# Moving the second layer's modulation out of the first layer's work queue, and dropping the zeroed accumulator banks of the scans

## The chip, the cores and the metric

One program runs on one core of one Trainium2 chip. The metric is device time in microseconds of a whole execution; lower is better. Below, PE is TensorE (matmuls), PEld its weight loads, DVE is VectorE, ACT is ScalarE, POOL is GpSimd, and SP is SyncE, whose queue issues almost all loads.

## The reference, cut to what matters

Two layers run over 256 context and 256 latent tokens of width 2048. Each layer modulates a normalised input, projects it, runs four token mixers (A and C are attention, B and D are bidirectional scans), merges them and projects back:

```
for l in range(2):
    shift, scale, gate = split(silu(c) @ w_mod[l] + b_mod[l], 3)     # the modulation; once more with c_ctx
    h = rms(x, norm_g[l]) * (1 + scale) + shift
    p = h @ w_in[l]
    y = [mixer_a(p), mixer_b(p), mixer_c(p), mixer_d(p)]             # B: RWKV scan, D: gated delta scan
    x = x + gate * (sum_i sigmoid(p_g @ g_up[l][i] + g_b[l][i]) * (y[i] @ w_br[l][i]) @ w_out[l])
return rms(x, final_g)
```

The modulation depends on c alone and not on x, so the second layer's may be computed at any time before it is used: shift and scale at the start of layer 1, gate at its end.

## The kernel before

Features lie on the 128 partitions in 16 tiles, the 512 tokens along the free axis. Products with big weights are done as three float32r matmuls of 128x128 by 512 columns: `weights` (L371) loads 256 KB into a "wr" buffer (5 of them) by SP, ScalarE casts it to "wh", VectorE takes the remainder "wl" (4 buffers each).

**Modulation.** `w_mod` of a layer is 12 chunks of 512 columns; chunks 0 to 3 give shift, 4 to 7 scale, 8 to 11 gate. `mod_unit` (L471) does one unit: four loads of 256 KB from `in_wmod`, and four float32 matmuls of 128x32 by 512 columns, each to another strip of 32 partitions of one bank. Sixteen units are a group of four chunks. With `acc` the group accumulates in one bank; without it each unit takes a new "big" bank and VectorE adds it to "ms". After the last unit four small matmuls and four additions put the result into `mod`.

**Order of the work.** Long products are generators in a queue. `small` (L259) is called for each matmul of the scans, adds its cost times `rho` to a debt, and pumps filler from the queue until the debt is paid. `rho` is from the table `RHO`, by layer and by stage (B or D). The filler of layer 0 is 45 projections (56, less the 11 that the first stage makes), then the merges of B, D, A and C, 16 output tiles each. `MODL` says which modulation units go along: for layer 0 the gate's 16 units of layer 0, and all 48 of layer 1. One unit is enqueued behind each projection (L437 to L441), the others run after every second tile of the merges (L1376). Both take "wr" buffers for their loads. The modulation for shift and scale of layer 0 runs in the first stage (`mods`, L1509), with 16 buffers "mr" of its own, between the first projections. Instructions stand on each engine's queue in an order fixed at build time, and each engine works its queue in that order. It isn't the order of the code throughout: work that is ready earlier can be put ahead.

**Output projection and boundary.** `out_proj` (L1381) splits the merged rows and then, for each of 16 tiles, loads x, runs 4 weight loads of 256 KB with 48 matmuls of 512 columns, adds the residual and (in layer 0) stores the latent half to `x1`. `rms_rows` (L514) then sums squares over the partitions and gives the row norms; `build_h` (L522) normalises and modulates the 16 tiles; three projections (Bw, Bk0, Bv0) start at once, a quarter of the 16 tiles at a time, in three banks.

**Scans.** Each of the 4 heads or head pairs of B and D accumulates its two directions in the one bank "acc". `zero_acc` (L326) opens that bank with a matmul of 512 columns by a tile of zeros, "zr", and all later matmuls add.

Of the kernel before, what the change touches and what calls it, by code (L numbers as in the profile page):

```python
# [9 lines left out]
F32 = mybir.dt.float32  # L10
F32R = mybir.dt.float32r
# [161 lines left out]
MXB = 3  # L173
NL2 = 3
MODS = (2, 3)
MODL = (((0, 8, 12), (1, 0, 12)), ())
NMAIN = 6
MORE = 5
STACK = (True, False)
PLAIN = ('', 'BA')  # L180
SIDE = (2.0, 1.8)
RHO = (((1.75,) * 4, (1.75,) * 4), ((1.8,) * 4, (1.4,) * 4))
QUANT = 2600.0
STEP = 1050.0
BG = (3, 3, 4, 10, 10)
# [2 lines left out]
class Kern:  # L188
# [134 lines left out]
    def tmp(s, n=512):  # L323
        return s.tl(s.rp, [128, T], "raw")[:, 0:n]

    def zero_acc(s):  # L326

        ps = s.psa.tile([128, 512], F32, tag="acc", name=s.nm("acc"))
        s.mm(ps, s.zr, s.zr[:, 0:1].to_broadcast([128, 512]), True, False)
        return ps  # L330

    def rsqrt(s, v, n):

# [97 lines left out]
    def enqueue_proj(s, names, mods=0):  # L431

        for name in names:
# [4 lines left out]
            for _ in range(mods):  # L438
                u = next(s.modq, None)
                if u is not None:  # L440
                    s.enqueue(u, s.mod_gen(u))  # L441

    def mod_gen(s, u):
        s.mod_unit(*u, [(s.wp, "wr")])
        return
        yield
# [21 lines left out]
        s.nc.vector.memset(s.s32, 0.0)  # L468
        s.ts(s.s32[:, :, 6:8], th, 0.5, None, ALU.mult)

    def mod_unit(s, l, chunks, u, pools, acc=False):  # L471


        nc = s.nc
        i, nch = u // 4, len(chunks)
        first, last = u == 0, u == 4 * nch - 1
        raws = []
        for g in range(4):
            pool, tag = pools[g % len(pools)]
            raw = s.tl(pool, [128, 512], tag)  # L480
            nc.sync.dma_start(raw, s.i["wmod"][l, chunks[i], u % 4 * 4 + g])
            raws.append(raw)
        if first or not acc:
            s.mps = s.big()
        ps = s.mps
        for g in range(4):
            s.mm(ps[32 * g:32 * g + 32, :], s.s32[:, u % 4 * 4 + g, 6 - 2 * i:38 - 2 * i], raws[g],
                 not acc or first, not acc or last)
        if last if acc else first:
            s.ms = s.tl(s.rp, [128, 512], "ms")  # L490
            nc.scalar.copy(s.ms, ps)
        elif not acc:
            s.tt(s.ms, s.ms, ps, ALU.add)
        if last:
            par, mod = s.lp[l]
            bo = _PO["bm"][0]
            w = 2 * nch
            p2 = s.big()
            for f in range(4):
                s.mm(p2[:, w * f:w * f + w], s.ms[:, f * 128:(f + 1) * 128], s.c("sel", 0, w))  # L500
            pv = p2[:, 0:4 * w].rearrange("p (f i c) -> p i f c", f=4, c=2)
            for i, n in enumerate(chunks):
                s.tt(mod[:, n * 4:n * 4 + 4, :], pv[:, i], wide(par[:, bo + n * 4:bo + n * 4 + 4], 2), ALU.add)
# [461 lines left out]
    def b_scan(s, J, d):  # L965
        nc = s.nc
        pool, t0 = s.bst["pool"], s.bst["t0"]
# [2 lines left out]
        vt = J["vt"]  # L970
        HS = (slice(0, 64), slice(64, 128))
        if d == 0:
            J["y"] = s.zero_acc()
        yps = J["y"]
        pc = None
        S = None
        for st in range(8):
# [28 lines left out]
            if c >= c0:  # L1006
                for R in HS:
                    o = yps[R, c * 64:c * 64 + 64]
                    s.mm(o, vt[R, c, :], AT[1][1][R, c, :], False, False)
                    if st > 0:  # L1010
                        s.mm(o, S[R, :], ar[R, c, 1, :], False, False)
                    s.mm(o, U[R, :], AT[0][1][R, c, :], False, d == 1 and st == 7)
# [231 lines left out]
    def d_scan(s, H):  # L1244
# [2 lines left out]
        k, kt, QD, sc, F = H  # L1247
        pool, t0 = s.dst["pool"], s.dst["t0"]
        m0 = t0 // 128
        ops_ = s.zero_acc()  # L1250
        S = [None, None]
        for st in range(4):
            ms = [s.ORDER2[d][st] for d in range(2)]
# [34 lines left out]
            for d, m in enumerate(ms):  # L1288
                if m >= m0:
                    o = ops_[:, tk[d]]  # L1290
                    if st > 0:
                        s.mm(o, S[d], sc[d][1][:, m * 128 - t0:m * 128 + 128 - t0], False, False)
                    s.mm(o, vn[d], QD[d][:, m - m0, :], False, d == 1 and st == 3)
            S = Sn
        return ops_

# [84 lines left out]
    def out_proj(s, xs_pool):  # L1381
# [10 lines left out]
            al.append(lo)  # L1392
        sqa = s.tl(xs_pool, [128, T], "sqa")[:, 0:n]
        xn = []
        for dt in range(KT):
            xo = s.tl(s.rp, [128, T], "po")[:, 0:n]
            nc.sync.dma_start(xo, s.i["xT"][dt] if l == 0 else s.x1[dt])
# [11 lines left out]
            s.sumsq(sqa, x, dt == 0)  # L1409
            if l == 0:  # L1410
                nc.sync.dma_start(s.x1[dt], x[:, CTX:])
            xn.append(x)
        return xn, sqa

# [7 lines left out]
    def open(s, ctx):  # L1422
# [9 lines left out]
        s.pss = ctx.enter_context(tc.tile_pool(name="pss", bufs=5 - MXB, space=MemoryType.PSUM))  # L1432
        s.psa = ctx.enter_context(tc.tile_pool(name="psa", bufs=1, space=MemoryType.PSUM))
        dr = ctx.enter_context(tc.tile_pool(name="dr", bufs=1, space=MemoryType.DRAM))
        s.zr = s.tl(s.cp, [128, 128], "zr0", F32R)
        z = s.tmp(128)
        s.nc.vector.memset(z, 0.0)
        s.nc.vector.tensor_copy(s.zr, z)
        s.cst = {}
        s.consts("cst", s.cp)  # L1440
        s.x1 = [dr.tile([128, CTX], F32, tag=f"x1_{k}", name=f"x1_{k}") for k in range(KT)]
# [43 lines left out]
    def run(s):  # L1485
        tc, nc = s.tc, s.nc
        with ExitStack() as ctx:
# [56 lines left out]
            for l in range(L):  # L1544
# [4 lines left out]
                with tc.tile_pool(name=f"xs{l}", bufs=1) as xp:  # L1549
                    xn, sqa = s.out_proj(xp)  # L1550
                    rsb = s.rms_rows(sqa, xp)
                    if l + 1 < L:
                        s.l = l + 1
                        s.par, s.mod = s.lp[l + 1]
                        s.build_h(xn, rsb)
                        names = ["Bw", "Bk0", "Bv0", "Br0", "Bk1"][:NL2]
                        banks = [s.bank() for _ in range(MXB)] + [s.scb((128, 512)) for _ in range(5 - MXB)]
                        s.filling = True
                        for g in range(4):
                            for ps, name in zip(banks, names):  # L1560
                                t0 = CTX if name[1] == "r" else 0
                                s.proj_part(ps[:, 0:T - t0], l + 1, name, t0, g)
                        for ps, name in zip(banks, names):
                            t0 = CTX if name[1] == "r" else 0
                            s.proj_park(ps[:, 0:T - t0], l + 1, name, t0)
                            s.done.add((l + 1, name))
# [22 lines left out]
```

## Time and profile before

| | us |
|---|---|
| median of 3 runs (2890.31 to 2902.11) | 2894.54 |
| the profiled execution | 2890.47 |
| its span | 2888.7 |
| PE busy, share of the span | 2740.9, 95% |
| DVE busy, share of the span | 1887.3, 65% |

The profiled execution is 1.8 us longer than its span, and 4.1 us under the median. In time order: the first stage to 174 us, layer 0's B scans to about 800, its D scans with both attentions to about 1395, the drain of merges to about 1541, the first output projection to 1735, the boundary to about 1790, then layer 1. Busy times are unions; two matmuls that overlap in the pipeline count once. A matmul's record is longer than the time it holds the engine, so costs are read from start to start.

### The profile page before, as it was taken

How to read it: one execution, taken by the hardware profiler on the slowest of the kernel's cores; microseconds unless marked ns; L12 is line 12 of the kernel's file. 1: busy time of each engine (PE TensorE's matmuls, PEld its weight loads, DVE VectorE, ACT ScalarE, POOL GpSimd, SP SyncE). 2: the span in 40 equal slices, each digit the busy share in tenths (PEclk: the TensorE clock that was granted, in tenths of full speed). 3: DMA queues.
4: the chain of work that ended last, by engine and by line, in shares of the span. 5: the costliest groups of instructions: out<-in, count | busy, mean ns of one | idle time of the engine just before them, and what ended most of it. 6: DMA issues, size and time to landing. Idle time of an engine off the chain costs nothing.

```text
span 2888.7 us, 52594 instructions
## 1 busy us (share of the span) xinstructions
PE 2740.9 (95%) x19454; PEld 2067.3 (72%) x19454; DVE 1887.3 (65%) x5302; ACT 1264.9 (44%) x2705; POOL 180.4 (6%) x436
## 2 busy tenths in 40 slices
PE   7998999999999999899999997999999999999897
PEld 3576566766667676666678886776777887877797
DVE  4337776656666767766555335777776677677775
ACT  3334333333244555555344225534433356455553
POOL 0000000000000101000000000001000001100000
PEclk9999999999999999999999998999999999899998
DMA  9753243433454434434634443323322453432465
GB/s 338 259 187 124 85 128 107 137 105 107 160 175 132 146 114 141 134 115 147 188 123 121 129 128 98 102 80 90 93 74 86 141 152 94 132 101 79 143 185 162
DMA packets 210049, 385.80 MB, mean 134 GB/s; under 512 B 24640, under 2 KB 37824, under 8 KB 209792
## 3 DMA queue, kind: packets, MB, share of 16 engines
q1 hardware_dynamic: 199872, 351.23, 39.6%
q0 software_dynamic: 9920, 31.20, 2.9%
q8 instruction: 153, 2.51, 0.4%
q14 instruction: 104, 0.85, 0.1%
HBM read 346.95 MB, written 35.39 MB: 132 GB/s over the span
## 4 chain that ended last, share of the span: by engine, by line
PE 71%; DVE 13%; ACT 5%; issue 5%; DMA 5%; POOL 0%; SPq 0%; DVEq 0%; ACTq 0%; POOLq 0%
PE big L283 47%; PE mx L283 12%; PE sc L283 6%; PE mx L305 3%; PE acc L283 3%; DVE wl L312 2%; DVE iX L312 1%; DMA wr<-in_win 1%; DVE it L312 1%; ACT raw L309 1%; ACT wh L376 1%; DVE raw L312 1%; DMA wr<-in_gup 1%; DMA wr<-in_wbr 1%; DMA po<-y 0%
## 5 line engine op out<-in xcount | busy, mean ns | idle before, releaser
L283 PE MATMUL big<-Rb,wh 128*128 128x512 f32 (+1 forms) x3280 | 1101.8, 365 | 14.7 <-ACT Rb L1317 5.5
L283 PE MATMUL big<-Ra,wh 128*128 128x512 f32 (+1 forms) x2128 | 780.5, 367 | 11.6 <-DVE po L315 7.7
L376 ACT CAST wh<-wr 128x512 fp32r<-128x512 f32 x712 | 438.4, 619 | 751.9 <-PE big L283 422.5
L283 PEld LDWEIGHTS big<-Rb,wh 128*128 128x128 f32 x3280 | 611.6, 192 | 119.3 <-ACT Rb L1317 9.9
L312 DVE TENSOR_TENSOR wl<-wr,wh 128x512 fp32r<-128x512 f32 x712 | 487.5, 688 | 286.9 <-ACT wh L376 276.5
L283 PE MATMUL big<-Ra,wl 128*128 128x512 f32 (+1 forms) x1616 | 595.2, 369 | 6.8 <-DVE wl L312 6.8
L283 PEld LDWEIGHTS big<-Ra,wh 128*128 128x128 f32 x2128 | 407.1, 191 | 106.7 <-issue 14.5
L283 PE MATMUL big<-Rb,wl 128*128 128x512 f32 (+1 forms) x1088 | 379.7, 349 | 0.9 <-DVE wl L312 0.9
L283 PEld LDWEIGHTS big<-Ra,wl 128*128 128x128 f32 x1616 | 309.5, 192 | 57.1 <-DVE wl L312 11.9
L283 PEld LDWEIGHTS big<-Rb,wl 128*128 128x128 f32 x1088 | 207.8, 191 | 26.6 <-DVE wl L312 1.8
L312 DVE TENSOR_TENSOR iX<-iX,it 128x60 f32<-128x60 f32 (+24 forms) x744 | 181.0, 243 | 15.5
L312 DVE TENSOR_TENSOR it<-iB,iX 128x60 f32<-128x60 f32 (+24 forms) x744 | 172.2, 231 | 15.3
L315 DVE SCALAR_TENSOR_TENSOR po<-po,big 128x512 f32<-128x512 f32 (+1 forms) x128 | 70.4, 550 | 81.3 <-PE big L283 72.9
L283 PE MATMUL big<-Rb,wr 128*128 128x256 f32 (+1 forms) x448 | 113.4, 423 | 5.0 <-DVE Ra L315 2.4
L309 ACT ACTIVATE po<-big,gb 128x512 f32<-128x512 f32 (+1 forms) x128 | 74.0, 578 | 93.8 <-PE big L283 79.9
L309 ACT ACTIVATE sw<-S,wc 128x64 f32<-128x64 f32 x96 | 33.4, 348 | 173.3 <-DVE S L315 149.7
L283 PE MATMUL big<-wr,s 128*32 128x512 f32 x512 | 97.4, 613 | 3.7 <-DVE ms L312 2.3
L283 PEld LDWEIGHTS big<-Rb,wr 128*128 128x128 f32 (+1 forms) x448 | 72.5, 182 | 25.9 <-issue 8.5
L283 PE MATMUL big<-mr,s 128*32 128x512 f32 x256 | 55.4, 638 | 17.8 <-DMA mr<-in_wmod 17.8
L283 PE MATMUL sc<-vt,AT 64*64 64x64 f32 x512 | 72.1, 238 | 0.0
L315 DVE SCALAR_TENSOR_TENSOR cz<-raw,par,cz 128x508 f32<-128x508 f32 (+3 forms) x96 | 67.1, 699 | 3.0 <-ACT cz L309 2.3
L626 DVE TENSOR_REDUCE mx<-mx 128x1 f32<-128x512 f32 (+1 forms) x96 | 57.1, 597 | 16.5 <-PE mx L283 15.2
(369 smaller groups left out, 4090.6 us busy)
## 6 DMA issues: line engine op xcount, KB each, us to landing
wr<-in_win SPq DMA_DIRECT2D x440, 256.0 KB, 2.7
wr<-in_wmod SPq DMA_DIRECT2D x256, 256.0 KB, 4.0
mr<-in_wmod SPq DMA_DIRECT2D x128, 256.0 KB, 5.2
wr<-in_wbr SPq DMA_DIRECT2D x128, 256.0 KB, 2.7
wr<-in_wout SPq DMA_DIRECT2D x128, 256.0 KB, 2.9
wr<-in_gup SPq DMA_DIRECT2D x64, 256.0 KB, 2.7
x<-in_xT SPq DMA_DIRECT2D x16, 256.0 KB, 5.4
po<-y SPq DMA_DIRECT2D x16, 256.0 KB, 3.3
```

Of the source, the lines that this page charges most:

```text
L283: s.nc.tensor.matmul(o, l, r, start=start, stop=stop)
L305: s.nc.tensor.transpose(o, i, s.c("id"))
L309: s.nc.scalar.activation(o, i, f, bias=bias, scale=scale, **k)
L312: s.nc.vector.tensor_tensor(o, a, b, op)
L315: s.nc.vector.scalar_tensor_tensor(o, a, sc, b, op0, op1)
L376: s.nc.scalar.copy(hi, raw)
L626: nc.vector.tensor_reduce(mx[:, hc], ps[:, 0:nk], AX.X, ALU.max)
```

## The change

- `MODL` keeps only the 16 units of layer 0's gate in the queue. The 48 units of layer 1 leave it.
- `next_mods` is a generator of these 48 units, in the order shift, scale, gate, all in the accumulating form, with "mr" buffers in the output projection's pool. Shift and scale take a bank of the "mx" pool, the gate one of the "big" pool.
- `out_proj` of layer 0 draws two units behind every tile, after the store of `x1`: 32 units, shift and scale.
- At the boundary eight units stand ahead of `build_h`, and two behind each of the four quarters of the first projections: 16 units, the gate.
- `zero_acc` becomes `acc_bank`: no matmul by zeros; the first matmul into the bank starts the accumulation. "zr" goes, with the instructions that make it.
- `RHO` for layer 0's D stage goes from 1.75 to 1.65.

```diff
--- before.py
+++ after.py
@@ -173,13 +173,13 @@
 MXB = 3
 NL2 = 3
 MODS = (2, 3)
-MODL = (((0, 8, 12), (1, 0, 12)), ())
+MODL = (((0, 8, 12),), ())
 NMAIN = 6
 MORE = 5
 STACK = (True, False)
 PLAIN = ('', 'BA')
 SIDE = (2.0, 1.8)
-RHO = (((1.75,) * 4, (1.75,) * 4), ((1.8,) * 4, (1.4,) * 4))
+RHO = (((1.75,) * 4, (1.65,) * 4), ((1.8,) * 4, (1.4,) * 4))
 QUANT = 2600.0
 STEP = 1050.0
 BG = (3, 3, 4, 10, 10)
@@ -323,11 +323,10 @@
     def tmp(s, n=512):
         return s.tl(s.rp, [128, T], "raw")[:, 0:n]
 
-    def zero_acc(s):
-
-        ps = s.psa.tile([128, 512], F32, tag="acc", name=s.nm("acc"))
-        s.mm(ps, s.zr, s.zr[:, 0:1].to_broadcast([128, 512]), True, False)
-        return ps
+    def acc_bank(s):
+
+
+        return s.psa.tile([128, 512], F32, tag="acc", name=s.nm("acc"))
 
     def rsqrt(s, v, n):
 
@@ -440,6 +439,13 @@
                 if u is not None:
                     s.enqueue(u, s.mod_gen(u))
 
+    def next_mods(s, pool):
+
+        for n in (0, 4, 8):
+            for u in range(16):
+                s.mod_unit(s.l + 1 if n < 8 else s.l, tuple(range(n, n + 4)), u, [(pool, "mr")], True, s.bank if n < 8 else None)
+                yield
+
     def mod_gen(s, u):
         s.mod_unit(*u, [(s.wp, "wr")])
         return
@@ -468,7 +474,7 @@
         s.nc.vector.memset(s.s32, 0.0)
         s.ts(s.s32[:, :, 6:8], th, 0.5, None, ALU.mult)
 
-    def mod_unit(s, l, chunks, u, pools, acc=False):
+    def mod_unit(s, l, chunks, u, pools, acc=False, bank=None):
 
 
         nc = s.nc
@@ -481,7 +487,7 @@
             nc.sync.dma_start(raw, s.i["wmod"][l, chunks[i], u % 4 * 4 + g])
             raws.append(raw)
         if first or not acc:
-            s.mps = s.big()
+            s.mps = (bank or s.big)()
         ps = s.mps
         for g in range(4):
             s.mm(ps[32 * g:32 * g + 32, :], s.s32[:, u % 4 * 4 + g, 6 - 2 * i:38 - 2 * i], raws[g],
@@ -495,7 +501,7 @@
             par, mod = s.lp[l]
             bo = _PO["bm"][0]
             w = 2 * nch
-            p2 = s.big()
+            p2 = (bank or s.big)()
             for f in range(4):
                 s.mm(p2[:, w * f:w * f + w], s.ms[:, f * 128:(f + 1) * 128], s.c("sel", 0, w))
             pv = p2[:, 0:4 * w].rearrange("p (f i c) -> p i f c", f=4, c=2)
@@ -970,7 +976,7 @@
         vt = J["vt"]
         HS = (slice(0, 64), slice(64, 128))
         if d == 0:
-            J["y"] = s.zero_acc()
+            J["y"] = s.acc_bank()
         yps = J["y"]
         pc = None
         S = None
@@ -1006,7 +1012,7 @@
             if c >= c0:
                 for R in HS:
                     o = yps[R, c * 64:c * 64 + 64]
-                    s.mm(o, vt[R, c, :], AT[1][1][R, c, :], False, False)
+                    s.mm(o, vt[R, c, :], AT[1][1][R, c, :], d == 0 and c == c0, False)
                     if st > 0:
                         s.mm(o, S[R, :], ar[R, c, 1, :], False, False)
                     s.mm(o, U[R, :], AT[0][1][R, c, :], False, d == 1 and st == 7)
@@ -1247,7 +1253,7 @@
         k, kt, QD, sc, F = H
         pool, t0 = s.dst["pool"], s.dst["t0"]
         m0 = t0 // 128
-        ops_ = s.zero_acc()
+        ops_, fresh = s.acc_bank(), True
         S = [None, None]
         for st in range(4):
             ms = [s.ORDER2[d][st] for d in range(2)]
@@ -1289,8 +1295,10 @@
                 if m >= m0:
                     o = ops_[:, tk[d]]
                     if st > 0:
-                        s.mm(o, S[d], sc[d][1][:, m * 128 - t0:m * 128 + 128 - t0], False, False)
-                    s.mm(o, vn[d], QD[d][:, m - m0, :], False, d == 1 and st == 3)
+                        s.mm(o, S[d], sc[d][1][:, m * 128 - t0:m * 128 + 128 - t0], fresh, False)
+                        fresh = False
+                    s.mm(o, vn[d], QD[d][:, m - m0, :], fresh, d == 1 and st == 3)
+                    fresh = False
             S = Sn
         return ops_
 
@@ -1392,6 +1400,8 @@
             al.append(lo)
         sqa = s.tl(xs_pool, [128, T], "sqa")[:, 0:n]
         xn = []
+        if l == 0:
+            s.modn = s.next_mods(xs_pool)
         for dt in range(KT):
             xo = s.tl(s.rp, [128, T], "po")[:, 0:n]
             nc.sync.dma_start(xo, s.i["xT"][dt] if l == 0 else s.x1[dt])
@@ -1409,6 +1419,8 @@
             s.sumsq(sqa, x, dt == 0)
             if l == 0:
                 nc.sync.dma_start(s.x1[dt], x[:, CTX:])
+                for _ in range(2):
+                    next(s.modn)
             xn.append(x)
         return xn, sqa
 
@@ -1432,10 +1444,6 @@
         s.pss = ctx.enter_context(tc.tile_pool(name="pss", bufs=5 - MXB, space=MemoryType.PSUM))
         s.psa = ctx.enter_context(tc.tile_pool(name="psa", bufs=1, space=MemoryType.PSUM))
         dr = ctx.enter_context(tc.tile_pool(name="dr", bufs=1, space=MemoryType.DRAM))
-        s.zr = s.tl(s.cp, [128, 128], "zr0", F32R)
-        z = s.tmp(128)
-        s.nc.vector.memset(z, 0.0)
-        s.nc.vector.tensor_copy(s.zr, z)
         s.cst = {}
         s.consts("cst", s.cp)
         s.x1 = [dr.tile([128, CTX], F32, tag=f"x1_{k}", name=f"x1_{k}") for k in range(KT)]
@@ -1552,6 +1560,8 @@
                     if l + 1 < L:
                         s.l = l + 1
                         s.par, s.mod = s.lp[l + 1]
+                        for _ in range(8):
+                            next(s.modn)
                         s.build_h(xn, rsb)
                         names = ["Bw", "Bk0", "Bv0", "Br0", "Bk1"][:NL2]
                         banks = [s.bank() for _ in range(MXB)] + [s.scb((128, 512)) for _ in range(5 - MXB)]
@@ -1560,6 +1570,8 @@
                             for ps, name in zip(banks, names):
                                 t0 = CTX if name[1] == "r" else 0
                                 s.proj_part(ps[:, 0:T - t0], l + 1, name, t0, g)
+                            for _ in range(2):
+                                next(s.modn)
                         for ps, name in zip(banks, names):
                             t0 = CTX if name[1] == "r" else 0
                             s.proj_park(ps[:, 0:T - t0], l + 1, name, t0)
```

## Rows read from the trace of the kernel before

**Rows 1.** The page: busy time by engine, and the last chain by engine.

```profile
PE 2740.9 (95%) x19454; PEld 2067.3 (72%) x19454; DVE 1887.3 (65%) x5302; ACT 1264.9 (44%) x2705; POOL 180.4 (6%) x436
...
PE 71%; DVE 13%; ACT 5%; issue 5%; DMA 5%; POOL 0%; SPq 0%; DVEq 0%; ACTq 0%; POOLq 0%
```

**Rows 2.** Busy in stretches: stretch, length, PE, PEld, DVE, ACT, POOL; clock, DMA share, GB/s.

```profile
800.00:1395.00 595.00, 562.10 (x3384) 408.69 (x3382) 420.17 (x1217) 306.67 (x706) 44.55 (x117) 0.98 0.44 138
1395.00:1541.00 146.00, 140.87 (x610) 106.45 (x611) 82.57 (x132) 57.28 (x92) 0.00 (x0) 0.99 0.47 146
1585.00:1735.00 150.00, 149.84 (x662) 123.73 (x660) 57.36 (x95) 42.85 (x69) 0.00 (x0) 1.00 0.43 130
1735.00:1768.00 33.00, 16.49 (x61) 13.08 (x61) 25.51 (x54) 25.84 (x52) 1.84 (x5) 0.69 0.10 31
```

**Rows 3.** Timeline, PE, layer boundary: start, length, engine, line, operation, [idle, releaser].

```profile
1745.79 0.80 PE L283 MATMUL mx<-Ra,wh 128*128 128x512 f32 x1 [3.53 <-ACT Ra L536]
...
1767.87 0.80 PE L283 MATMUL mx<-Ra,wh 128*128 128x512 f32 x1 [8.36 <-ACT wh L376]
...
1771.45 0.53 PE L283 MATMUL mx<-Ra,wl 128*128 128x512 f32 x1
```

**Rows 4.** Timeline, PE: units among scan matmuls and between projections.

```profile
570.27 1.06 PE L283 MATMUL big<-wr,s 128*32 128x512 f32 x8
571.27 0.33 PE L283 MATMUL sc<-vt,AT 64*64 64x64 f32 x2
...
764.63 1.07 PE L283 MATMUL big<-wr,s 128*32 128x512 f32 x8
...
777.20 1.06 PE L283 MATMUL big<-wr,s 128*32 128x512 f32 x8
```

**Rows 5.** Timeline, PE and DVE: merges with units (first two) and without.

```profile
1426.91 1.07 PE L283 MATMUL big<-wr,s 128*32 128x512 f32 x8
...
1436.95 1.06 PE L283 MATMUL big<-wr,s 128*32 128x512 f32 x8
...
1507.76 0.69 DVE L315 SCALAR_TENSOR_TENSOR po<-po,big 128x512 f32<-128x512 f32 x1 [0.73 <-PE big L283]
...
1511.84 0.69 DVE L315 SCALAR_TENSOR_TENSOR po<-po,big 128x512 f32<-128x512 f32 x1 [0.49 <-PE big L283]
```

**Rows 6.** Instructions on tile "ms": form, count, shortest, median, longest in ns.

```profile
L312 DVE TENSOR_TENSOR ms<-ms,big x60: 661/684/690, 251.3 to 1448.4; 128x512 f32<-128x512 f32 x60
```

**Rows 7.** Timeline, PE, first stage: units with buffers of their own.

```profile
110.06 1.06 PE L283 MATMUL big<-mr,s 128*32 128x512 f32 x8
...
114.00 1.07 PE L283 MATMUL big<-mr,s 128*32 128x512 f32 x8
```

**Rows 8.** Stretches, instructions on tile "s": PE, PEld, DVE; clock, DMA share, GB/s.

```profile
0.00:73.00 73.00, 28.26 (x104) 4.97 (x104) 0.75 (x2) 0.98 0.95 338
73.00:146.00 73.00, 19.68 (x104) 3.01 (x104) 0.00 (x0) 1.00 0.74 253
```

**Rows 9.** Timeline, SP's queue, first output projection.

```profile
1606.42 7.57 SPq L373 DMA_DIRECT2D wr<-in_wout  x4
1616.10 0.33 SPq L1411 DMA_DIRECT2D x<-x  x1
```

**Rows 10.** Timeline, PE: a bank of zeros and the matmul after it.

```profile
795.12 0.46 PE L283 MATMUL acc<-zr 128*128 128x512 f32 x1
795.41 0.39 PE L283 MATMUL big<-Ra,wh 128*128 128x512 f32 x1
```

**Rows 11.** Busy time of instructions on tile "big" in the D stage.

```profile
800.00:1395.00 595.00, 402.17 (x1622) 255.71 (x1620) 45.63 (x73) 30.97 (x48) 0.98 0.44 138
```

**Rows 12.** Loads of modulation weights: who waited for them; time to landing.

```profile
  PEld big L283: 11.3, 24
DMA to landing us min/median/max: 2.5/4.2/6.7
```

## Prediction

> **What bounds the kernel now.** I read the page first. TensorE (PE) is busy 95% of the span, and the chain that ended last lies on it for 71%; no other engine passes 72% [rows 1]. A share is a mean, so next came the busy time by stretch. In the first output projection PE is busy 149.84 of 150 us, 662 matmuls of 512 columns or 0.226 us each: that stretch is full. In the stretch with the D scans and both attentions PE is busy 562 of 595 us, in the drain of merges behind it 141 of 146 us. The layer boundary is the exception: 16.49 of 33 us, at a granted clock of 0.69 and a DMA share of 0.10 [rows 2]. PE's timeline shows why: after the last output tile PE waits for the row norms, does a burst of projections, then stands 8.36 us while ScalarE is still normalising the next tiles [rows 3]. What the change takes from the full stretches therefore comes back; what it puts into the output projection is paid; what it puts into the boundary may be free.
>
> **Units taken out of layer 0.** A modulation unit is 4 loads of 256 KB and 4 column-tiled matmuls, 8 records. 64 run in layer 0 from the queue: one behind each of 45 projections, 19 inside the merges. 48 of them (29 and 19) are the second layer's and leave.
> Price of one between projections: two units start 12.57 us apart with one projection of 48 matmuls between them [rows 4]. 48 x 0.2267 is 10.88, so the unit and what it upsets cost 1.69 us. It takes four of the five "wr" buffers, and the next weights come late. Where small scan matmuls stand on both sides, the unit costs only its own 1.00 us [rows 4]. Most lie between these, so I take 1.4: 29 x 1.4 = 40.6 us.
> Price of one in a merge: in the drain two units start 10.04 us apart, around two output tiles; without units one tile takes 4.08 us [rows 5]. So 10.04 - 8.16 = 1.88 us. Six of the 19 run in that drain (two stand in the rows): 11.3 us. The other 13 run beside scans and attention, where part of the upset meets other waits; I take 1.4, 18.2 us.
> Together 70 us back. Bounds: 48 x 1.00 = 48, and 29 x 1.69 + 19 x 1.88 = 84.7 us. VectorE also loses 45 of its 60 additions into "ms" at 0.684 us [rows 6], 31 us of an engine that isn't the bound; where PE waits for one, it is already in the 1.69 and 1.88, so nothing more is counted.
>
> **Units put into the output projection.** Two per output tile, 32 in all. They use 16 buffers of their own ("mr"), leave "wr" to the weights, and accumulate in one bank, so no addition follows each. The first stage has this form, one unit after every 12 or 24 matmuls: 3.94 us from unit to unit with 12 matmuls between [rows 7], so 3.94 - 2.72 = 1.22 us, with nothing upset behind it. In a pair the second saves the changes of tile form: 1.00 by [rows 4]. So 16 x 2.22 = 35.5 us. Bounds: 32 x 1.00 = 32, and 32 x 1.88 = 60 if they upset the weights as in the merges.
> The cover for their loads: each tile moves 1 MB of weights and 2 MB for units, some 0.4 MB of x besides. That is 3.5 MB in about 13.1 us, 267 GB/s. In the first stage the engines moved 253 GB/s at a share of 0.74, and 338 at most [rows 8]; I take the loads as hidden. Each load is also an issue on SP, which carries the weights and the store of x1. Over one tile SP issues four weight loads in 7.57 us and is then held for the next store [rows 9]; eight more issues of 0.33 us are 2.6 us of a period of 13. The end of each chunk group adds a copy, 8 small matmuls and 4 additions, as it did before in the queue: zero.
>
> **Units put into the boundary.** Eight ahead of the normalised tiles and eight between the projections. At 1.0 to 1.22 they are 16 to 19.5 us against 16.5 us of idle PE [rows 2]. Besides, the 8 intervals from 1767.87 to 1771.45 took 3.58 us, 0.45 each, which is the 1.2 GHz level, where 1.81 would do at 2.4 GHz [rows 3]; a PE with units in its gaps may skip this once or twice, 1.8 to 3.5 us back. Against it: only 4 units have buffers, so 12 or more of the 16 load after the last output tile, at 3.1 us each by 338 GB/s [rows 8], some 40 us beside the 55 us that the boundary lasts. New waits: a unit whose data is late holds every matmul behind it on PE, the norm statistics and projections among them; a load that waits for a buffer holds SP, and with it "win" weights and the first loads of layer 1. I take +4 us (a few units uncovered), bounds -3.5 (all covered, clock held) and +19.5 (none).
>
> **Bank of zeros.** Eight scans per layer open with one matmul of 512 columns; it holds PE 0.29 us from its start to the next and lasts 0.46 [rows 10]. 16 x 0.29 = 4.6 us back, bounds 3.6 (16 x 0.2267) and 7.4. The first real matmul now waits for the bank, later than the zeros did: zero.
>
> **Spacing 1.75 to 1.65 in the D stage.** 5.7% less filler per scan step. Work in "big" is 402 us there [rows 11], so up to 23 us of it moves into the drain. While the scans get shorter with it, it costs 0, which I take, since PE is busy 94% there and the drain keeps over 100 us; if every step only waits instead, 23 us. The sum of PE work doesn't change, so I exclude a gain.
>
> **Sum.** -70 + 35.5 + 4 - 4.6 + 0 = -35 us. From the profiled execution's 2890.5 us that is 2855; it lies 4 us under the median of the runs shown, and I add half of that: 2857 us. A change under 0.5%, about 14 us, can't be told from none.
>
> **Rivals.**
> *More comes back.* All units give the upper price, gaps and clock are won: -84.7 + 32 - 3.5 - 7.4 = -64, 2827 us. For it: the 1.69 and 1.88 are the only clean measurements. Against: many units stand among scan matmuls.
> *The boundary isn't filled.* The units stand on PE behind the waits they should fill: +19.5 in place of +4, 2870 us. For it: four units' buffers only. Against: DMA share 0.10 there.
> *Transfers pace the output projection.* Weights arrive late behind 2 MB of units per tile, 1.88 each: 60 in place of 35.5, and half the boundary uncovered: -70 + 60 + 10 - 4.6 = -5, 2886 us, no difference. For it: 267 GB/s is above the 253 of [rows 8]. Against: 338 were moved.
> *Slower, by SP's order.* The unit loads follow the store of x1 in the code, and the store waits for the tile's last matmul. If they also stand behind it in SP's queue, and the units ahead of the next tile's matmuls on PE, each tile waits for a landing, 4.2 us in the median [rows 12]: 16 x 4.2 = 67, -35 + 67 = +32, 2922 us. It decides from 2.2 us a tile (35/16). Against: the next tile's weights run ahead of that store already, or PE couldn't be full [rows 2], and 16 buffers reach two tiles ahead. In the first stage such loads held PE's weight loads 11.3 us in 24 waits, 0.47 us each [rows 12].
> *Slower, because PE isn't the bound.* If the scans' latencies set the pace up to 1395 us, only the six units in the drain return: -11 + 35.5 + 4 - 4.6 = +24, 2914 us. Against: PE idles only 33 of 595 us beside the scans, and 402 of its 562 busy us are filler [rows 2, 11]. The Trainium skill (Perfetto Trace Analysis, Identifying the Most-Contended Engine) speaks for it: matmul busy time says little of the distance to the limit, the busy share of weight loads should be used. By that rule the 72% for weight loads would leave over a quarter free. The trace disagrees in the output projection, where weight loads are busy 124 of 150 us and yet no matmul could start earlier.
>
> **How the numbers follow.** Forecast, 2840 to 2870 or so: 0.60. More comes back: 0.08. Boundary unfilled: 0.10. Transfers: 0.12. SP's order: 0.06. Scans: 0.04. Faster by over 0.5%: 0.60 + 0.08 + 0.10 = 0.78; within: 0.12; slower: 0.10. The range leaves out the two slower cases and the outermost part of the others: 2830 to 2888 us.
>
> **What would show it.** Drain tiles at 4.08 us without a break; output tiles some 2.2 us longer than 10.88, with no wait on "mr" above 0.5 us; the idle 16.5 us of the boundary mostly filled, its length within 5 us of now; 16 matmuls on "zr" gone. It is wrong if output tiles take over 15.3 us (10.88 + 2.2 + 2.2), if the first projections of layer 1 wait for loads, or if PE's idle time beside the D scans grows by what the units took.

## The result, and the profile of the changed kernel

The changed kernel takes 2846.72 us in the median of four runs (2842.45 to 2847.23), beside 2898.32 for four runs of the kernel before. The ratio on record is 0.9831, interval 0.9805 to 0.9857; the two medians alone give 0.9822. Run again later it gave 2844.64, ratio 0.9855 (0.9825 to 0.9886). With the experiments the kernel before took 2891.38 to 2892.36 in the median, so the change is worth 45 to 52 us. Its profiled execution took 2842.45 us, 48.0 less than that of the kernel before. Predicted were 2857 us, 35 less in the sum, range 2830 to 2888.

The page hardly shows it: TensorE (PE) is busy the same share, and VectorE has 47 instructions less and 30 us of work less [rows 1].

```profile
PE 2710.4 (95%) x19438; PEld 2056.8 (72%) x19438; DVE 1856.9 (65%) x5255; ACT 1260.0 (44%) x2705; POOL 180.0 (6%) x436
```

Three marks cut the execution better: the end of the first and of the last output tile (the starts of the first and of the last addition of the residual, the two times in the VectorE row) and the issue of layer 1's first load, behind which nothing of the change is left but eight banks of zeros, and the last two gate units. First the two rows of the kernel before, then those of the changed one.

```profile
L315 DVE SCALAR_TENSOR_TENSOR x<-big,mod,po x32: 473/480/486, 1571.7 to 1735.3; 128x256 f32<-128x256 f32 x32
```

```profile
1790.91 0.33 SPq L451 DMA_DIRECT2D raw<-p_Bw  x1
```

```profile
L315 DVE SCALAR_TENSOR_TENSOR x<-big,mod,po x32: 474/480/487, 1481.3 to 1674.4; 128x256 f32<-128x256 f32 x32
```

```profile
1740.65 0.33 SPq L457 DMA_DIRECT2D raw<-p_Bw  x1
```

| stretch, us | before | after | difference | by the prediction's terms |
|---|---|---|---|---|
| start to the end of the first output tile | 1571.7 | 1481.3 | -90.4 | -70 - 2.3 + 0 |
| to the end of the last output tile | 163.6 | 193.1 | +29.5 | +33.3 (15 pairs) |
| to layer 1's first load | 55.6 | 66.25 | +10.6 | +6.2 (last pair, boundary) |
| layer 1's rest | 1097.8 | 1100.05 | +2.3 | -2.3 |

So layer 0 gave back 18 us more than forecast, the output projection cost 4 less and the boundary 4 more. But the 4 us are no cheaper pairs. By their records three and a quarter of the 32 units run in the drain already, ahead of the first mark, since work that is ready earlier can be put ahead; most of them are these:

```profile
1401.87 1.92 PE L283 MATMUL mx<-mr,s 128*32 128x512 f32 x14
...
1408.50 1.07 PE L283 MATMUL mx<-mr,s 128*32 128x512 f32 x8
```

So between the two marks stand 13 pairs and three quarters of a unit, not 15 pairs. The price of a pair is read from tile to tile, before and after:

```profile
1636.96 0.88 DVE L315 SCALAR_TENSOR_TENSOR x<-big,mod,po 128x256 f32<-128x256 f32 x2 [1.56 <-PE big L283]
1647.84 0.88 DVE L315 SCALAR_TENSOR_TENSOR x<-big,mod,po 128x256 f32<-128x256 f32 x2 [1.56 <-PE big L283]
```

```profile
1556.17 0.88 DVE L315 SCALAR_TENSOR_TENSOR x<-big,mod,po 128x256 f32<-128x256 f32 x2 [1.55 <-PE big L283]
1569.17 0.88 DVE L315 SCALAR_TENSOR_TENSOR x<-big,mod,po 128x256 f32<-128x256 f32 x2 [1.55 <-PE big L283]
```

A tile takes 13.00 us instead of 10.88: 2.12 a pair. The 29.5 us are about 13 x 2.12, 1.22 for the three strips behind the second tile, and 0.90 for the small matmuls at the end of a group of chunks. Three stretches of the changed kernel: D scans with both attentions, output projection, boundary (columns as in [rows 2]).

```profile
822.10:1329.10 507.00, 483.25 (x2981) 378.85 (x2980) 382.51 (x1142) 289.80 (x682) 42.26 (x113) 0.98 0.29 89
...
1481.30:1674.40 193.10, 193.10 (x950) 140.29 (x951) 63.74 (x109) 47.64 (x77) 0.00 (x0) 1.00 0.78 257
1674.40:1740.65 66.25, 65.55 (x284) 31.21 (x277) 32.05 (x64) 33.02 (x65) 0.54 (x1) 1.00 0.78 266
```

The same for the boundary of the kernel before, between its marks, and what PE waited for in it (total, times, longest):

```profile
1735.30:1790.91 55.61, 39.40 (x154) 31.84 (x155) 32.99 (x65) 32.79 (x63) 2.92 (x7) 0.79 0.24 70
```

```profile
PE mx L283 <- ACT wh L376: 8.4, 1, 8.4
PE mx L283 <- ACT Ra L536: 3.5, 1, 3.5
```

Beside the D scans PE idles 24 of 507 us, no more than the 33 of 595 before [rows 2]. PE does not idle in the output projection; the transfers move 257 GB/s there. The boundary is filled, 65.6 of 66.3 us at a granted clock of 1.00 (2.4 GHz throughout) where it was 39.4 of 55.6 at a mean of 0.79, the 1.2 GHz level behind the long waits [rows 3], and yet it is longer. PE's timeline shows with what it is filled:

```profile
1689.01 0.39 PE L283 MATMUL mx<-Ra,wh 128*128 128x512 f32 x1
1689.24 0.40 PE L283 MATMUL mx<-Rb,wh 128*128 128x512 f32 x1
1689.56 1.04 PE L283 MATMUL big<-mr,s 128*32 128x512 f32 x2
1690.54 0.50 PE L283 MATMUL mx<-Rb,wh 128*128 128x512 f32 x1
...
1723.11 1.07 PE L283 MATMUL big<-mr,s 128*32 128x512 f32 x8
1724.11 0.50 PE L283 MATMUL mx<-Ra,wh 128*128 128x512 f32 x1
```

A unit is 8 records, two for each strip. At 1723.11 one runs whole and holds PE 1.00 us. At 1689.56 a single strip runs, between projections, and holds it 0.98. Between 1685.8 and 1717.9 there are, besides one whole pair, 16 such pieces, 11 of one strip and 5 of two: 21 strips, 5.25 units, for 16 x 0.98 = 15.7 us, where 5.25 whole units would take 5.3.

In the output projection the pair runs as one piece. Neither PE nor its weight loads wait on "mr" there; the profile does put 10.5 us of ScalarE's and 8.1 us of VectorE's waits for weights down to these loads, which PE, being full, doesn't feel:

```profile
1555.74 0.39 PE L283 MATMUL big<-Rb,wl 128*128 128x512 f32 x1
1556.06 1.92 PE L283 MATMUL mx<-mr,s 128*32 128x512 f32 x16
1557.91 0.50 PE L283 MATMUL big<-Rb,wh 128*128 128x512 f32 x1
```

On SP's queue the store of `x1` stands between the loads of one unit and the next, with the weights behind them:

```profile
1544.13 0.33 SPq L487 DMA_DIRECT2D mr<-in_wmod  x1
1544.56 1.39 SPq L1421 DMA_DIRECT2D x<-x  x1
1546.04 3.25 SPq L487 DMA_DIRECT2D mr<-in_wmod  x7
1549.34 0.42 SPq L1407 DMA_DIRECT2D po<-in_xT  x1
1549.86 5.11 SPq L372 DMA_DIRECT2D wr<-in_wout  x4
```

And the drain of merges has its plain tiles, 4.08 us apart [rows 5], but for a step of 9.9 us about 1405, where the early units stand:

```profile
1379.95 0.69 DVE L315 SCALAR_TENSOR_TENSOR po<-po,big 128x512 f32<-128x512 f32 x1 [2.19 <-PE big L283]
...
1384.03 0.69 DVE L315 SCALAR_TENSOR_TENSOR po<-po,big 128x512 f32<-128x512 f32 x1 [1.59 <-PE big L283]
```

### The profile page after: what moved, and what is told of

Read it like the earlier page. It is cut to its first block, busy times and chain, and to the rows that moved or that the text cites. A ratio compares the mean times of both kernels' runs of the same rounds, so it can differ in the third digit from the quotient of the medians.

```text
span 2840.7 us, 52626 instructions
## 1 busy us (share of the span) xinstructions
PE 2710.4 (95%) x19438; PEld 2056.8 (72%) x19438; DVE 1856.9 (65%) x5255; ACT 1260.0 (44%) x2705; POOL 180.0 (6%) x436
## 5 line engine op out<-in xcount | busy, mean ns | idle before, releaser
L312 DVE TENSOR_TENSOR iX<-iX,it 128x60 f32<-128x60 f32 (+24 forms) x744 | 181.4, 244 | 15.7
L312 DVE TENSOR_TENSOR it<-iB,iX 128x60 f32<-128x60 f32 (+24 forms) x744 | 172.7, 232 | 15.6
L283 PE MATMUL big<-mr,s 128*32 128x512 f32 x384 | 85.2, 617 | 18.3 <-DMA mr<-in_wmod 18.3
L309 ACT ACTIVATE po<-big,gb 128x512 f32<-128x512 f32 (+1 forms) x128 | 74.2, 579 | 57.3 <-PE big L283 41.2
L283 PE MATMUL sc<-vt,tok 64*64 64x64 f32 x448 | 67.5, 232 | 0.0
```

The lines of the kernel that those rows point to most:

```text
L283: s.nc.tensor.matmul(o, l, r, start=start, stop=stop)
L309: s.nc.scalar.activation(o, i, f, bias=bias, scale=scale, **k)
L312: s.nc.vector.tensor_tensor(o, a, b, op)
```

## Experiments

Theory at their start: a unit in the queue costs more than the prediction took, by what its loads and additions do to others; in the output projection and at the boundary it costs its matmuls. Rivals: the extra gain comes from the bank of zeros or the spacing; or the units' cost is PE's own time. Each kernel was timed beside the kernel before; its marks come from the profile of one of its executions.

**Price of the units in their old places.**

```diff
-MODL = (((0, 8, 12), (1, 0, 12)), ())
+MODL = (((0, 8, 12),), ())
```

> The kernel before without the second layer's 48 modulation units (its modulation is a constant, so that part of the computation is missing). This prices those units where they stood, with spacing and bank of zeros unchanged. The prediction's price, 70 us, gives 2828 us against the 2898 of the kernel before; its upper bound, 84.7, gives 2813. The trace of the changed kernel, whose layer 0 reaches the output projection 90.5 us earlier, speaks for 85 to 88 us, 2811. If the scans' latencies set the pace, only the drain's six units return: 2887. The output projection should stay at 174 us and the boundary at 56.

2807.74 us, ratio 0.97 (0.9676 to 0.9724): 84.6 us less than the 2892.36 beside it. The first output tile ends at 1479.0, 92.7 us earlier; output projection 163.6 (15 tiles; the 174 expected counts 16), boundary 56.4.

```profile
L315 DVE SCALAR_TENSOR_TENSOR x<-big,mod,po x32: 474/480/486, 1479.0 to 1642.6; 128x256 f32<-128x256 f32 x32
```

By the marks a unit in the queue cost 1.93 us, by the medians 1.76. In the profiles the difference lies in layer 1, 1108 us here against 1097.8 for the same code (below). Either way it is at the prediction's upper bound or over it, and the rival in which the scans' latencies set the pace is out. Of the 92.7 us, 59.7 come back between the end of the attentions and the first output tile's end, most of it the drain: the queue pays a debt, so what a unit takes beside a scan is missing at the queue's end. The kernel before, and this one:

```profile
1376.20:1571.70 195.50, 190.22 (x834) 145.00 (x832) 112.95 (x180) 78.89 (x129) 0.54 (x1) 0.99 0.46 142
```

```profile
1343.20:1479.00 135.80, 134.66 (x589) 109.33 (x586) 80.85 (x129) 59.91 (x99) 0.54 (x1) 1.00 0.36 108
```

**Price of the units in their new places.** `next_mods` of the changed kernel yields without a unit.

> The changed kernel without the same 48 units (the second layer's modulation is a constant). This prices them where they stand now. By the two traces the output projection should be 174 us again in place of 203.5, and the boundary 56 in place of 66.8: 40 us less, 2807 us. The prediction's terms, 35.5 + 4, give the same 40. If the units in the output projection only use time that weights would wait anyway, less than 32 returns there. Against the kernel before without the units it differs by the bank of zeros and the spacing alone: 4.6 us faster by the prediction.

2797.57 us, ratio 0.9664 (0.9634 to 0.9694), 47 to 49 us under the changed kernel's two medians. Its marks:

```profile
L315 DVE SCALAR_TENSOR_TENSOR x<-big,mod,po x32: 474/480/487, 1479.0 to 1642.5; 128x256 f32<-128x256 f32 x32
```

First tile 1479.0, output projection 163.5, boundary 55.7, layer 1 1100.0. So the units cost 2.3 us ahead of the first tile's end, 29.6 in the output projection, and 10.5 at the boundary with the last pair. The first tile ends at the same 1479.0 as without the units in the old kernel: zeros and spacing bring nothing there together. Of the 10 us between the two medians the profiles show 8 in layer 1. Eight zeros stand there, but layer 1 differs by as much between kernels that all have them (below), so this pair doesn't price them.

**The bank of zeros alone.**

```diff
-        s.mm(ps, s.zr, s.zr[:, 0:1].to_broadcast([128, 512]), True, False)
```

> The kernel before with only the bank of zeros gone (the scans' first matmul opens the bank). The prediction's 16 x 0.29 us gives 4.6 us less, ratio 0.9984. Rival: layer 1 of the changed kernel, which contains no other part of the change but eight zeros less, was not shorter (1100.05 against 1097.8 us), so the matmuls lay in gaps and the change is worth 0, ratio 1.000.

2896.76 us, ratio 1.0008 (0.9992 to 1.0024). The 0.9984 of the prediction lies outside. Between -2.3 and +7 us is left; no gain is seen. Nor is there one in the marks: the first tile ends at 1574.0, 2.3 us later.

**The spacing alone.**

```diff
-RHO = (((1.75,) * 4, (1.65,) * 4), ((1.8,) * 4, (1.4,) * 4))
+RHO = (((1.75,) * 4, (1.75,) * 4), ((1.8,) * 4, (1.4,) * 4))
```

> The changed kernel with the spacing of layer 0's D stage back at 1.75. The prediction took 0 for the spacing with bounds 0 to 23 us against it. If 0 holds, 2847 us, ratio to the changed kernel 1.000. If the smaller spacing is what brings the part of the 90.5 us that the units' prices don't explain, this is 5 to 20 us slower than the changed kernel; if it costs, up to 20 us faster.

2838.15 us, ratio 0.9805 (0.9781 to 0.9829), which overlaps with the changed kernel's. Its profile:

```profile
823.80:1338.90 515.10, 496.83 (x3027) 390.46 (x3027) 389.33 (x1155) 294.94 (x692) 40.14 (x113) 0.97 0.29 91
1338.90:1477.40 138.50, 137.76 (x611) 110.92 (x609) 81.83 (x132) 60.16 (x99) 0.54 (x1) 1.00 0.49 153
```

At 1.65 the D stage is 507.0 us instead of 515.1 and the stretch from the end of the attentions to the first tile's end 152.2 instead of 138.5. So the filler moved to the drain, as the prediction had it. The first tile ends 3.9 us earlier at 1.75; another pair of kernels, below, has it the other way (1482.1 at 1.75, 1479.1 at 1.65). The medians of both pairs are lower at 1.75, by 6 to 9 us (2838.15 against 2846.72 or 2844.64, and 2833.57 against 2839.65), with overlapping intervals. No gain by 1.65 is seen; whether it costs a few us stays open.

**What makes a queued unit dear.** Three kernels, the one before with the second layer's units stripped. The loads:

```diff
+            if l == 1:
+                raws.append(s.s32.rearrange("p a b -> p (a b)")[:, 0:512])
+                continue
```

> The kernel before, its 48 units of the second layer in their old places, but their matmuls read a tile that is always there: no loads of w_mod for them, no wr buffers (so the second layer's modulation is left wrong). All 48 together cost 92.7 us up to the first output tile by the traces with and without them, 1.93 each. If what they upset is the weights' buffers, only the 1.00 us of matmuls and the additions remain: some 45 us back, 2848 us. If the cost is PE's own time, the additions or the clock, nothing comes back: 2892.

2888.05 us, ratio 0.998 (0.9962 to 0.9997): 3.9 us less, between 0.9 and 11.

```profile
L315 DVE SCALAR_TENSOR_TENSOR x<-big,mod,po x32: 474/480/486, 1556.1 to 1719.7; 128x256 f32<-128x256 f32 x32
```

First tile at 1556.1: 15.6 us earlier, 0.33 a unit. Mark and median disagree; the profiled execution, 2875.45 us, is the shortest of the ten. Neither comes near 45: that the upset is above all the weights' buffers falls.

The additions:

```diff
-        elif not acc:
+        elif not acc and l == 0:
             s.tt(s.ms, s.ms, ps, ALU.add)
```

> The kernel before without the 45 additions into ms of the second layer's units (its modulation is left wrong); loads and matmuls stay. The prediction counted these additions at nothing beyond the upset: 0 to 5 us less. If VectorE's additions stand in the way of the scans' chains and of the big banks, 45 x 0.684 = 31 us come back, 2861.

2882.43 us, ratio 0.997 (0.9949 to 0.9991): 9.6 us less, between 2.6 and 15.

```profile
L315 DVE SCALAR_TENSOR_TENSOR x<-big,mod,po x32: 474/480/487, 1559.7 to 1723.2; 128x256 f32<-128x256 f32 x32
```

First tile at 1559.7: 12.0 us earlier, 0.25 a unit, neither nothing nor 31.

Both:

> The kernel before with the second layer's 48 units as bare matmuls: neither their loads nor their additions (the second layer's modulation is left wrong). Taken singly these brought the first output tile's end from 1571.7 to 1556.1 (loads) and 1559.7 us (additions), and leaving out the units brings 1479.0. If the two prices add up, 1544 us: 65 us, 1.36 a unit, is then what a lone unit holds PE, with its changes of form. If loads and additions cover for each other, so that only both together free the buffers and banks, down to 1530 (1.07 a unit, the 1.09 that one holds PE in the drain).

2862.79 us, ratio 0.9908 (0.9875 to 0.994): 28.6 us less, between 17 and 36.

```profile
L315 DVE SCALAR_TENSOR_TENSOR x<-big,mod,po x32: 474/481/486, 1543.5 to 1707.1; 128x256 f32<-128x256 f32 x32
```

First tile at 1543.5: by the marks the two prices add up (15.6 + 12.0 = 27.6, 28.2 seen), and 64.5 us remain, 1.34 a bare unit. By the medians the two alone come to 13.5 of the 28.6, which would mean that they partly cover for each other. Each mark is one execution's, and kernels with nearly the same code up to the first tile end it up to 5 us apart (1477.4 and 1482.1 above), so the total of both is shown and its division isn't. The drain shows a ladder, if only in part. Unit to unit over two tiles was 10.04 us [rows 5]; without loads, and then with neither:

```profile
1391.66 1.06 PE L283 MATMUL big<-s 128*32 128x512 f32 x8
...
1401.43 1.06 PE L283 MATMUL big<-s 128*32 128x512 f32 x8
```

```profile
1411.45 1.06 PE L283 MATMUL big<-s 128*32 128x512 f32 x8
...
1420.84 1.06 PE L283 MATMUL big<-s 128*32 128x512 f32 x8
```

9.77 and 9.39. Less two tiles, 8.16, a unit there is 1.88 whole, 1.61 without its loads, 1.23 bare. The last is the 1.22 that the prediction read in the first stage [rows 7]: a lone unit with buffers of its own and no addition. These are the usual distances; the kernel with loads and no additions has 10.01, 11.50 and 9.39 there and gives no step of its own.

**The boundary: strips or transfers.** One load of 1 MB for each unit, into one buffer.

```diff
+            r4 = s.tl(pools[0][0], [128, 4, 512], "m4")
+            nc.sync.dma_start(r4, s.i["wmod"][l, chunks[i], u % 4 * 4:u % 4 * 4 + 4].rearrange("k p n -> p k n"))
+            raws = [r4[:, g, :] for g in range(4)]
```

> The changed kernel, each of the 48 units loaded by one transfer of 1 MB into one buffer (4 such buffers, the same memory) in place of four of 256 KB, so that the four strips of a unit become ready together. If the boundary's 10.6 us are strips that run one by one as each lands (0.98 us for one, as much as for four together), the boundary falls to about 3 us over that of the kernel before, 59 us in place of 66.3, and the kernel is some 7 us faster than the changed one; the output projection stays. If the boundary is paced by the transfers themselves or by ScalarE's normalising, nothing changes: 66 us.

2839.65 us, ratio 0.9821 (0.9805 to 0.9838). The boundary, and two of its pieces:

```profile
1672.30:1730.42 58.12, 53.61 (x283) 31.27 (x276) 31.99 (x64) 33.00 (x64) 0.54 (x1) 0.97 0.85 306
```

```profile
1692.12 1.06 PE L284 MATMUL big<-m,s 128*32 128x512 f32 x8
...
1695.64 1.06 PE L284 MATMUL big<-m,s 128*32 128x512 f32 x8
```

58.1 us, as expected: whole units, with as many bytes, moved faster (306 GB/s). That the transfers' own speed was the limit doesn't fit: with four loads PE was busy for 65.55 of the 66.25 us, and with one it is busy for 53.61 and idles 4.5. Less the last pair (2.1) it is 0.4 us over the 55.6 of the kernel before, so the other units there now cost next to nothing. The median is 7.1 us below the changed kernel's first, as expected, and 5.0 below its second, with overlapping intervals; the profile's layer 1 is 7 us longer, 1107.3.

**All units in the output projection.**

```diff
-                for _ in range(2):
+                for _ in range(3):
                     next(s.modn)
```

> The changed kernel with all 48 units in the output projection, three behind each tile, and none at the boundary. Three units cost 2.22 + 1.0 by the prediction's terms: the output projection should be 16 us longer than in the changed kernel and the boundary 10.6 shorter, so 5 us slower, 2852. Rival: 4.5 MB per tile are more than the transfers bring in 14 us (310 GB/s needed, 248 to 282 seen): then tiles wait, over 16 us each, and it is 20 us slower or more.

2849.7 us, ratio 0.9857 (0.9842 to 0.9873). Output projection 207.8, boundary 57.3:

```profile
1482.80:1690.60 207.80, 207.80 (x1082) 145.31 (x1084) 63.93 (x115) 48.18 (x78) 0.00 (x0) 1.00 0.88 307
```

```profile
1521.33 0.88 DVE L315 SCALAR_TENSOR_TENSOR x<-big,mod,po 128x256 f32<-128x256 f32 x2 [1.55 <-PE big L283]
1535.16 0.88 DVE L315 SCALAR_TENSOR_TENSOR x<-big,mod,po 128x256 f32<-128x256 f32 x2 [1.55 <-PE big L283]
```

A tile takes 13.83 us, 2.95 over 10.88: a third unit costs 0.83 us. The median is 3 us above the changed kernel's 2846.72, where 5 were expected. Transfers of 307 GB/s at a share of 0.88 don't hold PE for a moment, and the rival of paced tiles falls even at three units.

**Towards a better version.** One load for each unit, spacing 1.75; the same with layer 0's own gate in the drain; and the changed kernel as their base.

```diff
-MODL = (((0, 8, 12),), ())
+MODL = ((), ())
...
+    def gate_gen(s, pool):
+        for u in range(16):
+            s.mod_unit(0, (8, 9, 10, 11), u, [(pool, "m4")], True, s.bank)
+            yield
```

> The changed kernel with one load for each unit and with the old spacing of 1.75. By the marks of the runs so far: first output tile 1477.4, output projection 193.5, boundary 58, layer 1 1100: 2829 us, against 2841 for the changed kernel's profile. If the 3.9 us of the spacing are chance, 2833.

2833.57 us, ratio 0.9809 (0.9781 to 0.9837). Marks: 1482.1, output projection 194.0, boundary 58.1, layer 1 1103.8.

> The same, and layer 0's own 16 gate units leave the queue for the drain of merges, one behind each output tile there, in buffers of their own and accumulating in one bank of the attention's, idle by then. If a unit in the queue costs 1.93 and a lone one in its own buffers 1.22, the first output tile ends 16 x 0.7 = 11 us earlier, 1466, and the kernel takes 2818 us. If tiles with a unit in the drain are paced by their transfers (1.4 MB in 5.3 us, 264 GB/s) or hold the weights' loads, the gain is gone: 2829 or more.

2835.02 us, ratio 0.9814 (0.9787 to 0.9841). First tile at 1472.0, 10.1 us before the one above, and its profile is 9 us shorter (span 2829.0 against 2838.0); in the drain a tile with a unit takes 5.30 us, 1.22 over a plain one:

```profile
1360.07 1.07 PE L284 MATMUL mx<-m,s 128*32 128x512 f32 x8
...
1365.37 1.06 PE L284 MATMUL mx<-m,s 128*32 128x512 f32 x8
```

So the stage did what was expected, but the profile above is the longest of its kernel's five executions and this one the shortest, and the medians show no gain: whether this move is worth anything stays open.

> The changed kernel itself once more, as the base for the two before it on the same chip. First output tile 1481.3, output projection 193.1, boundary 66.3, layer 1 1100 in its first profile: 2841 us. What layer 1, which is the same code in all of these, differs by between two executions of one kernel shows how much of a difference is chance: 1097.7 to 1108 us in the kernels so far.

2844.64 us, ratio 0.9855 (0.9825 to 0.9886); marks 1481.9, 193.1, 66.1, layer 1 1101.6. The version with one load for each unit is 11 us faster than this in the median, of which the boundary's 8 us are shown; their intervals overlap.

**How much is chance.** Layer 1 is the same code in all kernels from the first load on, but for the zeros. It took 1097.7 to 1108.0 us, with and without zeros alike. One stretch of 100 us, as long after the first load in the changed kernel and in the one with single loads:

```profile
2340.65:2440.65 100.00, 89.39 (x712) 75.66 (x712) 79.61 (x247) 56.17 (x136) 11.10 (x31) 0.95 0.35 109
```

```profile
2330.42:2430.42 100.00, 94.23 (x702) 78.67 (x703) 74.63 (x227) 55.34 (x135) 10.55 (x30) 0.87 0.32 100
```

The granted clock, a mean over its two levels, is 0.95 in one and 0.87 in the other, and PE is busy longer for as many matmuls. The clock differs with it; what makes it differ wasn't tried. The timings of the kernel before go the same way: 2877.35 us at a mean granted clock of 0.981, 2906.1 at 0.971. Differences below some 10 us of the span are therefore read from marks, which are single executions' themselves.

## Why the prediction came out as it did

**Units out of layer 0: right in kind, the term too small.** 70 us were forecast, 84.6 to 92.7 measured. The step that failed is the price among scans. "Where small scan matmuls stand on both sides, the unit costs only its own 1.00" read the distance from the unit's start to the next matmul's [rows 4]. It leaves out the change of form ahead of it (0.32 us from the last matmul's start to the unit's, where 0.23 is usual) and all that the unit does elsewhere. From there came the 1.4 for 42 of 48 units. Measured, the mean is 1.93 by the marks: 1.34 bare, and 0.59 by loads and additions together. With the drain's six at 1.88 the 42 come to an estimated 1.94. The clean rows, 1.69 and 1.88, were the better estimate, as the rival with more gain said. Its 2827 us were not reached, because the boundary cost 8.5 where it took 3.5 as won, and the zeros' 7.4 didn't come.

**What the upset is: half wrong.** The prediction blamed late weights behind four of five "wr" buffers and counted the additions at nothing. Loads and additions together are 28 us by mark and median alike, about a third of the price. The larger part, 1.34 of 1.93, stays with the bare matmuls: it is PE's own time, the rival named at the start. By the marks they weigh nearly the same, 15.6 and 12.0 us; the medians give 3.9 and 9.6, so how the 28 divide isn't settled. Why 1.34 remains over the 1.23 of the drain (5 us in 48 units) stays open; it is as large as the scatter.

**Units in the output projection: right.** 2.22 a pair was forecast, 2.12 measured from tile to tile. The end of a chunk group, taken as zero, cost 0.90 in this stretch. The cover held: full PE, 257 GB/s, no wait of PE on "mr". SP's order behind the store of `x1`, the slower rival, didn't occur: 16 buffers reach ahead, so that loads held behind the store by 1.4 us are early enough.

**Units at the boundary: right that the idle time fills and the clock holds, wrong in the mechanism of the cost.** +4 was taken, with "a few units uncovered"; 8.5 us is measured (66.25 - 55.6 - 2.1 for the last pair), inside the bounds. No unit was uncovered in the sense meant: PE waits 0.7 us in all. The step that failed is that a unit's price is the same however its strips come. Each strip has a load of its own, the strips stand apart in PE's order, and a lone strip takes as long as four side by side. The kernel with one load for each unit shows it, 58.1 for 66.25; that the strips stand apart because their loads land one after the other is the likely reading, argued and not tried by itself. The Trainium skill (TensorEngine Tiling (Array Packing), Tiling Modes) states that tiles run in parallel and that a change of tiling mode drains TensorE first; the trace fits both, 1.00 us for four strips beside 0.98 for one, and 0.32 us ahead of a unit where 0.23 is usual.

**Bank of zeros: wrong.** 4.6 us were forecast, with 3.6 as the least; the measured interval ends at 2.3. The price was the engine's time at one place [rows 10]. By the sum's own logic it should have come back from a full PE; that it doesn't show says that these matmuls lay where PE would have waited, or that scatter hides half of it. In the trace of the kernel before, four of the 16 are followed by a wait of PE for something else (0.5 to 1.4 us), but eleven hold it 0.22 to 0.85 us with no wait beside them, 4.5 us in all. So the first explains only a part, and the rest stays open.

**Spacing: not contradicted.** 0 was taken, with a cost of up to 23 us as the bound. The marks differ by 3 to 4 us in both directions; by the medians 1.65 may cost 6 to 9 us.

**Scans as the bound.** This rival, with the rule in its support that the Trainium skill gives (Perfetto Trace Analysis, Identifying the Most-Contended Engine), would have left 2914 us. 48 units taken out gave back 1.76 to 1.93 us each, so the traces stand against it in layer 0 too: in the changed kernel weight loads are busy 379 of the 507 us beside the D scans, which by the rule leaves a quarter free, and PE idles 24.

**Sum.** -18 us in layer 0 beyond the forecast, -4 in the output projection (units that ran ahead of it), +4 at the boundary, +4.6 in layer 1 (zeros and chance): -13, which is the difference between -48 and -35. The errors in size partly cancel: with only the price of the units in layer 0 put right, 92.7 for 70, the sum would have been -58, ten off on the other side. That part of the nearness is luck.

## What to carry over

Price a filler unit from two repeats of the whole pattern, with and without it, and not from its own start to the next start: what its loads, its additions and its changes of tile form do to others came to nearly as much again as its own time here. Count in the trace which units run in the stretch, too: some run earlier than the code says. Put such units side by side, with buffers and an accumulating bank of their own: 1.93 us became 1.06 in pairs and 0.98 in threes. Let matmuls that could run side by side become ready together, by one transfer, or each holds the engine for all.

## Unexpected on the chip

- A matmul on one strip of 32 columns between projections held PE 0.98 us, two strips 0.98, four side by side 1.00.
- Filling the boundary's gaps kept the granted clock at 1.00 where it was 0.79, and still cost time, since what filled them was dearer than the gaps.
- In the output projection with three units a tile, transfers at 307 GB/s, a share of 0.88 of the DMA engines, left PE busy for 207.8 of 207.8 us.
- The same code of layer 1 took 1097.7 to 1108.0 us in different kernels.
